# A DoRA forward pass on one core: the last stores awaited behind the closing barriers, rounding and copies in pairs, and a TensorE loop of half a block

## Chip, cores and metric

The kernel runs on one core of a Trainium2 chip. The metric is the device time of one execution in microseconds; lower is better. Four of the core's engines compute: TensorE (PE), VectorE (DVE), ScalarE (ACT) and GpSimd (POOL). SyncE (SP) issues the large transfers. "Span" is the time from the first to the last instruction of the program in a trace; every timed execution has a time and a span, and the difference ("time outside the span") matters below.

## The reference

```python
def setup_inputs():
    batch, seq_len, in_dim, out_dim = 16, 2048, 256, 256
    rank = 16
    ...
def reference(x, W, lora_A, lora_B, m, scale):
    W_adapted = W + scale * (lora_A @ lora_B)
    W_norm = np.sqrt(np.sum(W_adapted ** 2, axis=0, keepdims=True) + 1e-8)
    W_final = W_adapted / W_norm * m
    x_flat = x.reshape(-1, in_dim)           # 32768 x 256 float32
    y = x_flat @ W_final                     # 32768 x 256 float32
    return y.reshape(batch, seq_len, out_dim).astype(np.float32)
```

x and y are 33.5 MB each. The weights are tiny and are prepared once.

## The kernel before

The rows are cut into 8 blocks of 4096 (4 MB). Five buffers hold blocks; a result overwrites its input and is stored from there. A block is 8 chunks of 512 rows. For a chunk, POOL rounds to bfloat16, PE transposes (two bfloat16 values carried as one float32), DVE copies the transposed chunk out of PSUM, PE multiplies by the final weights, and ACT copies the product over the input.

SyncE issues all large loads and stores on one queue:

```python
    for b in range(XBUFS):                       # XBUFS = 5
        load_x(b)
    for b in range(NBLK):                        # NBLK = 8
        nc.sync.wait_ge(sem("done"), b + 1)
        nc.sync.dma_start(out=rows(out_flat, b), in_=x_bufs[b % XBUFS][:]).then_inc(
            sem(f"store{b}"), 16
        )
        if b >= 1 and b - 1 + XBUFS < NBLK:
            nc.sync.wait_ge(sem(f"store{b - 1}"), 16)
            load_x(b - 1 + XBUFS)
    for b in range(NBLK - XBUFS, NBLK):
        nc.sync.wait_ge(sem(f"store{b}"), 16)
    # ... [cut] after this: the closing barriers of the framework
```

A barrier is a meeting of the five engines: each signals that it has come, and waits until all have. In the trace of this kernel all five have semaphore events on the line of the closing barriers (L303), from 163.5 to 164.3 us.

POOL and DVE have one instruction per chunk (64 each); TensorE loops over blocks:

```python
    for g in range(NCH):                         # 64 chunks
        ... # [cut] waits
        nc.gpsimd.tensor_copy(out=xb_bufs[g % NXB][:],
            in_=x_bufs[b % XBUFS][:, c * J : (c + 1) * J, :]).then_inc(sem("rounded"), 1)
    # ... [cut]
    with nc.Fori(0, NBLK, 1, engines=[PE], head_slot={PE: 0}):
        turned(0)                                # 4 transposes
        for c in range(CH):                      # 8 chunks
            if c + 1 < CH:
                turned(c + 1)
            product(c)                           # 8 matmuls
```

## Time and profile before

| | before |
|---|---|
| time, median of the first three runs | 166.26 us (166.16 to 166.46) |
| span in the trace | 164.3 us |
| moved by DMA | 67.45 MB |
| busiest engine (PE) | 61% |
| last compute ends; last store issued | 139.6 us; 139.7 us |
| last store has landed | 162.8 us |

The page of the kernel before. Part 2 has one digit per fortieth of the span, 9 for 90% busy or more; below it are the GB/s of each slice.

```profile
span 164.3 us, 2075 instructions
PE 99.7 (61%) x778; PEld 83.9 (51%) x778; DVE 51.2 (31%) x76; ACT 66.8 (41%) x67; POOL 66.2 (40%) x70
...
DMA  5998999989999999999999999999999999999960
GB/s 199 415 479 383 499 391 415 479 383 495 399 399 359 399 479 401 439 439 399 479 407 439 447 399 457 433 423 455 407 431 439 423 463 399 439 447 407 471 295 16
...
q8 instruction: 1, 0.02, 0.0%
q14 instruction: 3, 0.02, 0.0%
...
L150 POOL CAST xb<-x_sb 128x1024 bf16<-128x1024 f32 x64 | 65.5, 1049 | 65.2 <-DMA x_sb<-in_x_dram 50.6
L184 DVE COPY xt<-xt_ps 128x512 f32<-128x512 f32 x64 | 43.9, 691 | 77.1 <-PE xt_ps L246 77.1
```

The DMA row stands at 8 or 9 from the second slice to the last but two, and no engine row (left out here) does. The "instruction" packets of q8 and q14 are taken to be fetches of the engines' own programs (called instruction fetches below): with TensorE's loop written out q8 has six packets in place of one, and with the main loops taken out it has none (late_unroll and dma_only, below). POOL and DVE wait for data for longer than DVE works. That is a kernel which moves bytes, and whose compute has time to spare.

SyncE's waits from 140 us on, in the kernel before (columns: total us, number, longest), and then its end by windows (us; only the last three columns matter: the granted clock of PE, the DMA engines' share, GB/s; a packet is counted whole in the window in which it starts, so a share can pass 1):

```profile
SPq L130 <- DMA out_dram<-x_sb: 22.8, 2, 13.1
SPq L303 <- PEq L303: 0.8, 2, 0.6
```

```profile
150.00:155.00 5.00, 0.00 (x0) 0.00 (x0) 0.00 (x0) 0.00 (x0) 0.00 (x0) 0.50 1.02 439
155.00:160.00 5.00, 0.00 (x0) 0.00 (x0) 0.00 (x0) 0.00 (x0) 0.00 (x0) 0.50 0.77 334
160.00:165.00 5.00, 0.00 (x0) 0.00 (x0) 0.00 (x0) 0.00 (x0) 0.00 (x0) 0.50 0.05 20
```

Three things stand here. SyncE does nothing but wait for stores up to 162.8 us. After that the barriers come (L303), in which nothing moves. And in the last 5 us the DMA engines are 5% busy: most are through by about 160 us, a few are not.

One view misleads. The chain that ended last begins and ends with compute, because its steps are compute instructions, and a store's landing is not one:

```profile
137.51 1.05 PE y_ps L258 x8
138.56 0.02 issue
138.58 1.01 ACT x_sb L201
```

It stops at 139.6 us and says nothing of the 25 us after. Where the end is a transfer, read the waits of SyncE instead.

The trace also records when each of the 16 parts of a transfer has landed. (One part per DMA engine: in this trace 16 packets are under way at a time, and 99% of those of 8 KB or more start within 4 ns of the end of an earlier one.) For the last store of the kernel before, in us:

```
159.39 159.52 159.63 159.64 159.65 159.75 159.75 159.89 159.94 159.97 160.04 160.10 160.12 160.31 162.55 162.80
```

Fourteen parts end within 0.9 us; two stragglers are 2.7 and 2.9 us behind the eighth. Below, "lag" is a part's landing minus that of the eighth part.

### The profile page before, as it was taken

The page shows a single profiled execution, that of the slowest core. Times are in us where ns is not written, and L with a number is a line of the kernel's source. Part 1 is how long each engine was busy: PE and PEld are TensorE (multiplying, and loading weights), DVE is VectorE, ACT ScalarE, POOL GpSimd, SP SyncE. Part 2 cuts the span into 40 slices and gives each one's busy share as a digit, 9 for nine tenths or more (in the row PEclk, how much of TensorE's full clock was granted, in tenths as well). Part 3 has the DMA queues.
Part 4 walks back from the last instruction along what each step waited for, and adds up shares of the span by engine and source line. Part 5 has one row for each costly group of instructions (what it writes and reads, how often), then busy time and mean ns, then how long its engine had stood idle before and what let it go on. Part 6 is the DMA issues. An engine that isn't in the chain of part 4 may idle for free. (4 is left out here: it accounts for less than half of the span.)

```text
span 164.3 us, 2075 instructions
## 1 busy us (share of the span) xinstructions
PE 99.7 (61%) x778; PEld 83.9 (51%) x778; DVE 51.2 (31%) x76; ACT 66.8 (41%) x67; POOL 66.2 (40%) x70
## 2 busy tenths in 40 slices
PE   1260899899899898994009993399704996000000
PEld 0120698798798796992007891279603895000000
DVE  0439355354453554451003450045301352000000
ACT  3010077577578577576000675027800377000000
POOL 1006859587785885800039600693007920000000
PEclk9999999999999999999555799579995799955555
DMA  5998999989999999999999999999999999999960
GB/s 199 415 479 383 499 391 415 479 383 495 399 399 359 399 479 401 439 439 399 479 407 439 447 399 457 433 423 455 407 431 439 423 463 399 439 447 407 471 295 16
DMA packets 2630, 67.45 MB, mean 410 GB/s; under 512 B 433, under 2 KB 450, under 8 KB 578
## 3 DMA queue, kind: packets, MB, share of 16 engines
q1 hardware_dynamic: 2448, 67.37, 95.9%
q10 hardware_dynamic: 178, 0.03, 0.1%
q8 instruction: 1, 0.02, 0.0%
q14 instruction: 3, 0.02, 0.0%
HBM read 33.85 MB, written 33.55 MB: 410 GB/s over the span
## 5 line engine op out<-in xcount | busy, mean ns | idle before, releaser
L150 POOL CAST xb<-x_sb 128x1024 bf16<-128x1024 f32 x64 | 65.5, 1049 | 65.2 <-DMA x_sb<-in_x_dram 50.6
L201 ACT COPY x_sb<-y_ps 128x1024 f32<-128x1024 f32 x64 | 64.8, 1013 | 64.5 <-PE y_ps L258 64.5
L258 PE MATMUL y_ps<-w_final,xt 128*128 128x256 bf16 x512 | 69.9, 282 | 3.9 <-PEq L235 3.6
L184 DVE COPY xt<-xt_ps 128x512 f32<-128x512 f32 x64 | 43.9, 691 | 77.1 <-PE xt_ps L246 77.1
L246 PE MATMUL xt_ps<-identity,xb 128*128 128x128 f32 x256 | 41.8, 295 | 28.4 <-PEq L235 28.4
L258 PEld LDWEIGHTS y_ps<-w_final,xt 128*128 128x128 bf16 x512 | 50.7, 101 | 14.7 <-issue 8.3
L246 PEld LDWEIGHTS xt_ps<-identity,xb 128*128 128x128 f32 x256 | 32.7, 153 | 31.4 <-issue 30.7
L223 PE MATMUL y_ps<-sq,ones 128*128 128x256 f32 x4 | 2.1, 674 | 1.6 <-DVE sq L169 1.6
L194 ACT ACTIVATE norm<-y_ps,eps_col 128x256 f32<-128x256 f32 x1 | 0.5, 474 | 5.9 <-PE y_ps L223 5.9
L212 PE MATMUL y_ps<-identity,a_nat 128*16 128x128 f32 x2 | 0.6, 396 | 3.6 <-DMA a_nat<-in_lora_A_dram 3.6
L180 DVE TENSOR_TENSOR w_final<-wam,rnorm 128x256 bf16<-128x256 f32 x2 | 2.3, 1200 | 0.0
L223 PEld LDWEIGHTS y_ps<-sq,ones 128*128 128x128 f32 x4 | 1.2, 323 | 2.3 <-DVE sq L169 2.1
L192 ACT ACT_TABLE_LOAD x1 | 1.3, 1283 | 2.4 <-issue 2.4
L212 PEld LDWEIGHTS y_ps<-identity,a_nat 128*16 128x16 f32 x2 | 0.1, 88 | 3.6 <-issue 3.6
L177 DVE RECIPROCAL rnorm<-norm 128x256 f32<-128x256 f32 x1 | 1.7, 1745 | 0.0
L171 DVE COPY m_all<-y_ps 128x256 f32<-128x256 f32 x1 | 0.4, 425 | 3.3 <-PE y_ps L228 3.3
L160 DVE CAST b_bf<-b_nat 16x256 bf16<-16x256 f32 x1 | 0.3, 281 | 3.6 <-DMA b_nat<-in_lora_B_dram 3.6
L216 PE MATMUL y_ps<-b_bf,aT 16*128 16x256 bf16 x2 | 0.6, 402 | 1.3 <-DVE aT L162 1.3
L228 PE MATMUL y_ps<-m_row,ones 1*128 1x256 f32 x2 | 1.2, 710 | 0.0
L216 PEld LDWEIGHTS y_ps<-b_bf,aT 16*128 16x128 bf16 x2 | 0.1, 104 | 1.8 <-DVE aT L162 1.8
L165 DVE SCALAR_TENSOR_TENSOR wa<-y_ps,w_nat 128x512 f32<-128x512 f32 x1 | 0.7, 692 | 0.8 <-PE y_ps L216 0.8
L228 PEld LDWEIGHTS y_ps<-m_row,ones 1*128 1x128 f32 x2 | 0.5, 308 | 0.7 <-issue 0.7
(12 smaller groups left out, 3.2 us busy)
## 6 DMA issues: line engine op xcount, KB each, us to landing
x_sb<-in_x_dram SPq DMA_DIRECT2D x8, 4096.0 KB, 29.3
out_dram<-x_sb SPq DMA_DIRECT2D x8, 4096.0 KB, 34.1
w_nat<-in_W_dram SPq DMA_DIRECT2D x1, 256.0 KB, 2.9
a_nat<-in_lora_A_dram ACTq DMA_DIRECT2D x1, 16.0 KB, 2.6
b_nat<-in_lora_B_dram ACTq DMA_DIRECT2D x1, 16.0 KB, 3.5
m_row<-in_m_dram ACTq DMA_DIRECT2D x1, 1.0 KB
```

What stands on the lines that cost most here:

```text
L150: nc.gpsimd.tensor_copy(out=xb_bufs[g % NXB][:], in_=x_bufs[b % XBUFS][:, c * J : (c + 1) * J, :],).then_inc(sem("rounded"), 1)
L165: nc.vector.scalar_tensor_tensor(out=wa[:], in0=ab_ps, scalar=float(scale), in1=w_nat[:], op0=ALU.mult, op1=ALU.add).then_inc(dv, 1)
L177: nc.vector.reciprocal(out=rnorm[:], in_=norm[:]).then_inc(dv, 1)
L180: i = nc.vector.tensor_mul(out=w_final[:, t], in0=wam[:, t], in1=rnorm[:])
L184: nc.vector.tensor_copy(out=xt_bufs[g % NXT][:].rearrange("p r t -> p (r t)").bitcast(FP32), in_=xt_ps[g % 4][:],).then_inc(sem("copied"), 1)
L192: nc.scalar.activation(out=warm[:], in_=eps_col[:], func=AF.Sqrt)
L201: nc.scalar.copy(out=x_bufs[b % XBUFS][:, c * J : (c + 1) * J, :], in_=y_ps[g % 2][:]).then_inc(sem("room"), 1)
L212: i = nc.tensor.transpose(aT_ps[:, t * P : (t + 1) * P], a_nat[:, t, :], identity[:])
L223: i = nc.tensor.matmul(n2_ps, ones[:], sq[:, t, :], start=(t == 0), stop=(t == KC - 1))
L228: nc.tensor.matmul(mb_ps, ones[0:1, :], m_row[:], start=True, stop=True).then_inc(pe, 1)
L246: i = nc.tensor.transpose(xt_ps[c % 4][:, j * P : (j + 1) * P], xb_bufs[c % NXB][:, j, :].bitcast(FP32), identity[:],)
L258: i = nc.tensor.matmul(y_ps[c % 2][:, j, :], xt_bufs[c % NXT][:, j * P : (j + 1) * P, t], w_final[:, t, :], start=(t == 0 and (j % (J // 2 ...
```

## The change

Its intent: the closing barriers and the semaphore clear take place under the last stores instead of after them, and POOL, DVE and TensorE need fewer, larger steps. The core of the diff:

```diff
-    ctx.enter_context(tc.tile_critical())
+    critical = ExitStack()
+    critical.enter_context(tc.tile_critical())
...
+    late = [nc.alloc_semaphore(f"store{b}") for b in range(NBLK - XBUFS, NBLK)]
+    sems = {f"store{b}": late[b - NBLK + XBUFS] for b in range(NBLK - XBUFS, NBLK)}
...
-    for b in range(NBLK - XBUFS, NBLK):
-        nc.sync.wait_ge(sem(f"store{b}"), 16)
...
-    for g in range(NCH):
+    for p in range(NPR):                     # 32 pairs of chunks
...
         nc.gpsimd.tensor_copy(
-            out=xb_bufs[g % NXB][:],
-            in_=x_bufs[b % XBUFS][:, c * J : (c + 1) * J, :],
+            out=xb_bufs[p % NXB][:],
+            in_=x_bufs[b % XBUFS][:, 2 * c * J : 2 * (c + 1) * J, :],
         ).then_inc(sem("rounded"), 1)
+    nc.gpsimd.wait_ge(sem("turned"), NPR - NXB + 1)
+    nc.gpsimd.memset(xb_bufs[NPR % NXB][:], 0.0).then_inc(sem("rounded"), 1)
... (DVE copies pairs likewise; two PSUM tiles of 1024 in place of four of 512)
-    with nc.Fori(0, NBLK, 1, engines=[PE], head_slot={PE: 0}):
+    turned(0)
+    with nc.Fori(0, NPR // 2, 1, engines=[PE], head_slot={PE: 96}):
+        turned(1)
+        product(0)
+        product(1)
         turned(0)
-        for c in range(CH):
-            if c + 1 < CH:
-                turned(c + 1)
-            product(c)
+    critical.close()
+    tc.close()
+    tc.compile()
+    for s in late:
+        nc.sync.wait_ge(s, 16)
+        nc.sync.sem_clear(s)
```

The loop now turns one pair more than there are (`turned(0)` at its end); POOL's `memset` gives it something to turn.

More of the change, by code (lines that the diff above doesn't have):

```diff
@@ L45 @@
     NCH = NBLK * CH
-    NXB = 4
-    NXT = 4
-    F4 = J * P
+    NPR = NCH // 2
+    PRB = CH // 2
+    NXB = 2
+    NXT = 2
+    F8 = 2 * J * P
     PE = mybir.EngineType.PE
-    ctx.enter_context(tc.tile_critical())
+    critical = ExitStack()
+    critical.enter_context(tc.tile_critical())
     def sb(name, shape, dtype):
@@ L62 @@
     x_bufs = [sb(f"x_sb{k}", [P, DJ, IN], FP32) for k in range(XBUFS)]
-    xb_bufs = [sb(f"xb{k}", [P, J, IN], BF16) for k in range(NXB)]
-    xt_bufs = [sb(f"xt{k}", [P, F4, KC], BF16) for k in range(NXT)]
+    xb_bufs = [sb(f"xb{k}", [P, 2 * J, IN], BF16) for k in range(NXB)]
+    xt_bufs = [sb(f"xt{k}", [P, F8, KC], BF16) for k in range(NXT)]
     w_nat = sb("w_nat", [P, KC, OUT], FP32)
@@ L82 @@
     w_final = sb("w_final", [P, KC, OUT], BF16)
-    xt_ps = [ps(f"xt_ps{k}", [P, F4], FP32) for k in range(4)]
+    xt_ps = [ps(f"xt_ps{k}", [P, F8], FP32) for k in range(2)]
     y_ps = [ps(f"y_ps{k}", [P, J, OUT], FP32) for k in range(2)]
@@ L90 @@
     mb_ps = y_ps[1][:, 2, :]
-    sems = {}
+    late = [nc.alloc_semaphore(f"store{b}") for b in range(NBLK - XBUFS, NBLK)]
+    sems = {f"store{b}": late[b - NBLK + XBUFS] for b in range(NBLK - XBUFS, NBLK)}
     def sem(name):
@@ L143 @@
     ).then_inc(sem("ident"), 1)
-    for g in range(NCH):
-        b, c = divmod(g, CH)
+    for p in range(NPR):
+        b, c = divmod(p, PRB)
         if c == 0:
             nc.gpsimd.wait_ge(sem(f"load{b}"), 16)
-        if g >= NXB:
-            nc.gpsimd.wait_ge(sem("turned"), g - NXB + 1)
+        if p >= NXB:
+            nc.gpsimd.wait_ge(sem("turned"), p - NXB + 1)
         nc.gpsimd.tensor_copy(
-            out=xb_bufs[g % NXB][:],
-            in_=x_bufs[b % XBUFS][:, c * J : (c + 1) * J, :],
+            out=xb_bufs[p % NXB][:],
+            in_=x_bufs[b % XBUFS][:, 2 * c * J : 2 * (c + 1) * J, :],
         ).then_inc(sem("rounded"), 1)
+    nc.gpsimd.wait_ge(sem("turned"), NPR - NXB + 1)
+    nc.gpsimd.memset(xb_bufs[NPR % NXB][:], 0.0).then_inc(sem("rounded"), 1)
     dv = sem("dve")
@@ L181 @@
     i.then_inc(dv, 1)
-    for g in range(NCH):
-        nc.vector.wait_ge(sem("turned"), g + 1)
+    for p in range(NPR):
+        nc.vector.wait_ge(sem("turned"), p + 1)
         nc.vector.tensor_copy(
-            out=xt_bufs[g % NXT][:].rearrange("p r t -> p (r t)").bitcast(FP32),
-            in_=xt_ps[g % 4][:],
+            out=xt_bufs[p % NXT][:].rearrange("p r t -> p (r t)").bitcast(FP32),
+            in_=xt_ps[p % 2][:],
         ).then_inc(sem("copied"), 1)
@@ L240, with turned @@
         j_order.append(a + J // 2)
-    def turned(c):
+    def turned(p):
         take("rounded")
-        for j in range(J):
+        for j in range(2 * J):
             i = nc.tensor.transpose(
-                xt_ps[c % 4][:, j * P : (j + 1) * P],
-                xb_bufs[c % NXB][:, j, :].bitcast(FP32),
+                xt_ps[p % 2][:, j * P : (j + 1) * P],
+                xb_bufs[p % NXB][:, j, :].bitcast(FP32),
                 identity[:],
@@ L251, in turned, with product @@
         i.then_inc(sem("turned"), 1)
-    def product(c):
+    def product(p):
         take("copied")
-        take("room")
-        for t in range(KC):
-            for j in j_order:
-                i = nc.tensor.matmul(
-                    y_ps[c % 2][:, j, :],
-                    xt_bufs[c % NXT][:, j * P : (j + 1) * P, t],
-                    w_final[:, t, :],
-                    start=(t == 0 and (j % (J // 2)) == 0),
-                    stop=(t == KC - 1 and (j % (J // 2)) == (J // 2) - 1),
-                )
-        i.then_inc(sem("product"), 1)
-    with nc.Fori(0, NBLK, 1, engines=[PE], head_slot={PE: 0}):
-        turned(0)
-        for c in range(CH):
-            if c + 1 < CH:
-                turned(c + 1)
-            product(c)
+        for h in range(2):
+            take("room")
+            for t in range(KC):
+                for j in j_order:
+                    r = (h * J + j) * P
+                    i = nc.tensor.matmul(
+                        y_ps[h][:, j, :],
+                        xt_bufs[p % NXT][:, r : r + P, t],
+                        w_final[:, t, :],
+                        start=(t == 0 and (j % (J // 2)) == 0),
+                        stop=(t == KC - 1 and (j % (J // 2)) == (J // 2) - 1),
+                    )
+            i.then_inc(sem("product"), 1)
+    turned(0)
[3 more added lines that the diff above has]
+        product(1)
+        turned(0)
+    critical.close()
[4 more added lines that the diff above has]
+        nc.sync.sem_clear(s)
 _INS = ['x', 'W', 'lora_A', 'lora_B', 'm', 'scale']
```

## The prediction

> **What bounds it now.** The DMA queues. The slice table has DMA at 8 or 9 tenths from 4 us to 160 us: 67.45 MB, mean 410 GB/s; 5 us windows show mostly 415 to 445 GB/s with or without compute beside them. In the landing records, the successive 4 MB transfers land 9.5 to 10.5 us apart. The engines are far below: PE 61%, ACT 41%, POOL 40%, DVE 31%. The last block's compute ends at 139.6 us (timeline), while the store that it releases can only begin to move when the store ahead is through, at about 150 us: 10 us of slack.
>
> **The tail.** SyncE waits for the last store until 162.8 us (waits of SP, L130). Then come the branch, two sets of barriers over five engines and a semaphore range clear of 0.24 us, to 164.3 us: 1.45 us in which nothing moves. About 1.9 us more of the 166.26 lie outside the span.
>
> **A second loss in the tail.** 14 of 16 engines have landed the last store by 160.3 us; two straggle to 162.55 and 162.80. The first lag (1.4 us) appears with the transfer during which the queue table's one "instruction" packet of q8 moved 16 KB (20.4 us); the second engine's lag grows from 53 us on, by about 0.3 us around each of the three 8 KB instruction fetches of q14 (65, 99 and 106 us).[...]
>
> **What the change does.**
> 1. Waits of the last stores behind the barriers: barriers and range clear run at about 140 us, under the stores. After the landing only a wait and a clear of SyncE remain, about 0.03 us each as the tail's waits show. Gain: 1.2 to 1.4 us, all on the critical path.
> 2. Pairs: 32 rounds of about 2.0 us (twice 1049 ns) and 32 copies of about 1.3 us (twice 691 ns). Pipeline steps get twice as coarse: the last block, 15.5 us from its load's landing to its last store's issue, should take 16 to 20 us, within its 25 us. Off the critical path: 0.
> 3. PE loop of 48 instead of 96 matmuls with the next pair turned ahead: PE is 61% busy: 0.
> 4. Side effect: shorter streams (half the POOL and DVE instructions, half the PE loop body), so fewer or earlier instruction fetches among the data. If the 16 KB fetch goes or moves before the loads, a straggler loses 1.4 us; but the other stays at about +2 us unless its fetches go too. I expect 0 to 1 us, 0.5 us in the middle.
>
> **Sum.** 166.26 - 1.35 - 0.5 = 164.4 us, 1.1% faster. Eight times in ten between 163.3 and 165.3. Chances: faster 0.06, same 0.93, slower 0.01.
>
> **What would show it.** SP's wait for the last store at the end, no barrier behind it; barriers near 140 us; end of span within 0.2 us of the last landing; POOL x32 at about 2.0 us, DVE x32 at about 1.3 us; compute end between 139 and 145 us. Step 4: fewer "instruction" packets, the stragglers closer to the other 14.
>
> **What would make it wrong.** The last block's compute later than about 150 us (PE at half clock throughout), which would open a gap before the last store; a straggler that grows instead; or time outside the span changing as SyncE ends last.

## The result, and the profile after

The median is 164.62 us (164.47 to 164.74, 4 runs) against 166.35 us (166.16 to 166.46, 4 runs) for the kernel before. The ratio is 0.9897, with a 95% interval of 0.9879 to 0.9914. A ratio here is the mean time of one kernel's fast runs over that of the other's of the same rounds, so it is not quite the ratio of the quoted medians.

The page of the changed kernel, the same lines:

```profile
span 163.3 us, 1983 instructions
PE 103.6 (63%) x786; PEld 84.2 (52%) x786; DVE 43.9 (27%) x44; ACT 63.6 (39%) x67; POOL 62.2 (38%) x39
...
DMA  5999998999999999999999999999999999999991
GB/s 201 394 490 401 425 470 385 482 417 393 482 409 361 401 401 482 401 450 433 409 466 409 401 490 393 442 452 401 474 409 393 474 409 433 458 401 474 409 393 48
...
q8 instruction: 1, 0.02, 0.0%
q14 instruction: 1, 0.01, 0.0%
...
L154 POOL CAST xb<-x_sb 128x2048 bf16<-128x2048 f32 x32 | 59.7, 1893 | 70.9 <-DMA x_sb<-in_x_dram 49.8
L191 DVE COPY xt<-xt_ps 128x1024 f32<-128x1024 f32 x32 | 38.1, 1221 | 86.6 <-PE xt_ps L253 86.6
```

Pairs save 5.8 us of POOL's rounding and 5.8 us of DVE's copying, and both engines simply wait longer (POOL's new memset takes 1.8 us of it back). SyncE's waits in the changed kernel from 143 us on, and its last windows:

```profile
SPq L129 <- ACTq L212: 19.9, 1, 19.9
SPq L289 <- DMA out_dram<-x_sb: 18.5, 2, 9.6
SPq L286 <- PEq L286: 0.7, 2, 0.5
```

```profile
150.00:155.00 5.00, 0.00 (x0) 0.00 (x0) 0.00 (x0) 0.00 (x0) 0.00 (x0) 0.50 0.99 426
155.00:160.00 5.00, 0.00 (x0) 0.00 (x0) 0.00 (x0) 0.00 (x0) 0.00 (x0) 0.50 0.77 334
160.00:165.00 5.00, 0.00 (x0) 0.00 (x0) 0.00 (x0) 0.00 (x0) 0.00 (x0) 0.50 0.06 26
```

The barriers (L286) now run at 143.3 to 144.6 us and the wait for stores (L289) comes last. The span ends 0.04 us after the last landing (163.28 and 163.24 us), where it ended 1.5 us after it before (164.31 and 162.80). The middle of the run is unchanged: the first part of the last store landed at 159.39 us in both traces. The chain of the changed kernel's trace is as blind as before; it ends with ACT's last copies:

```profile
139.89 1.05 PE y_ps L267 x8
140.93 0.02 issue
140.96 1.93 ACT x_sb L208 x2
```

The last block took 18.4 us from its load's landing (124.51 us) to its store's issue (142.94 us), against 15.6 us before, and nothing came of it.

Two things didn't fit, though the total did. The last straggler landed 0.44 us later than before (163.24 against 162.80 us), not earlier, and a third part lagged in this trace (161.77 us). And the span fell by 1.0 us between the two traces while the median time fell by 1.7 us. (In the two traced executions alone the time fell by 1.35 us, from 166.09 to 164.74 us, so only a part of the 0.7 us lies outside the span; the means below put it at 0.36 us.) These two were the questions for the experiments.

### The profile page after: what moved, and what is told of

It is laid out like the page before. It is cut to its first block, busy times and chain, and to the rows that moved or that the text cites. A ratio compares the mean times of both kernels' runs of the same rounds, so it can differ in the third digit from the quotient of the medians.

```text
span 163.3 us, 1983 instructions
## 1 busy us (share of the span) xinstructions
PE 103.6 (63%) x786; PEld 84.2 (52%) x786; DVE 43.9 (27%) x44; ACT 63.6 (39%) x67; POOL 62.2 (38%) x39
## 5 line engine op out<-in xcount | busy, mean ns | idle before, releaser
L208 ACT COPY x_sb<-y_ps 128x1024 f32<-128x1024 f32 x64 | 61.7, 1014 | 71.7 <-PE y_ps L267 71.7
L154 POOL CAST xb<-x_sb 128x2048 bf16<-128x2048 f32 x32 | 59.7, 1893 | 70.9 <-DMA x_sb<-in_x_dram 49.8
L267 PE MATMUL y_ps<-w_final,xt 128*128 128x256 bf16 x512 | 63.3, 276 | 13.4 <-PEq L242 13.4
L267 PEld LDWEIGHTS y_ps<-w_final,xt 128*128 128x128 bf16 x512 | 47.8, 99 | 28.0 <-issue 19.9
L191 DVE COPY xt<-xt_ps 128x1024 f32<-128x1024 f32 x32 | 38.1, 1221 | 86.6 <-PE xt_ps L253 86.6
L253 PE MATMUL xt_ps<-identity,xb 128*128 128x128 f32 x264 | 38.7, 307 | 20.0 <-PEq L242 20.0
L253 PEld LDWEIGHTS xt_ps<-identity,xb 128*128 128x128 f32 x264 | 34.5, 159 | 22.8 <-issue 22.6
L160 POOL MEMSET xb<- 128x2048 bf16 x1 | 1.8, 1804 | 3.8 <-PE xt_ps L253 3.8
L187 DVE TENSOR_TENSOR w_final<-wam,rnorm 128x256 bf16<-128x256 f32 x2 | 0.8, 422 | 0.0
```

The lines of the kernel that those rows point to most:

```text
L154: nc.gpsimd.tensor_copy(out=xb_bufs[p % NXB][:], in_=x_bufs[b % XBUFS][:, 2 * c * J : 2 * (c + 1) * J, :],).then_inc(sem("rounded"), 1)
L160: nc.gpsimd.memset(xb_bufs[NPR % NXB][:], 0.0).then_inc(sem("rounded"), 1)
L187: i = nc.vector.tensor_mul(out=w_final[:, t], in0=wam[:, t], in1=rnorm[:])
L191: nc.vector.tensor_copy(out=xt_bufs[p % NXT][:].rearrange("p r t -> p (r t)").bitcast(FP32), in_=xt_ps[p % 2][:],).then_inc(sem("copied"), 1)
L208: nc.scalar.copy(out=x_bufs[b % XBUFS][:, c * J : (c + 1) * J, :], in_=y_ps[g % 2][:]).then_inc(sem("room"), 1)
L253: i = nc.tensor.transpose(xt_ps[p % 2][:, j * P : (j + 1) * P], xb_bufs[p % NXB][:, j, :].bitcast(FP32), identity[:],)
```

## The experiments

Theory 1: the late waits are the whole gain, in two parts, the barriers inside the span and something outside the span that the other four engines do while SyncE still waits. Rivals: pairs and the shorter loop bring a part of the gain through shorter programs or fewer instruction fetches. For the stragglers the theory was that an instruction fetch of TensorE takes time from one DMA engine; the rivals were compute in general, and the DMA engines themselves.

The first four ran on one chip in the same rounds. All outputs were correct unless stated.

### Late waits alone (late_only)

```diff
 # the kernel before, with only:
-    for b in range(NBLK - XBUFS, NBLK):
-        nc.sync.wait_ge(sem(f"store{b}"), 16)
 ... (at the end, as in the change)
+    critical.close(); tc.close(); tc.compile()
+    for s in late:
+        nc.sync.wait_ge(s, 16); nc.sync.sem_clear(s)
```

> The kernel before with only the waits for the last five stores moved behind the closing barriers. Theory 1 (the late waits are the whole gain): ratio to before 0.988 to 0.991, about 164.5 us, the span ends within 0.1 us of the last landing, and time minus span falls from about 1.95 us to about 1.45 us as in the changed kernel. Rival (pairs and the shorter loop bring a part of it, through shorter programs or fewer instruction fetches): only the barriers' 1.4 us come off, ratio about 0.992 or more, time minus span stays at about 1.95 us.

Measured: 164.32 us (164.03 to 164.63, 4 runs), ratio 0.9889 (0.9867 to 0.9910). Theory 1 held. SyncE's waits in its trace have the barriers ahead of the stores, as in the changed kernel, and its last landing is at 162.68 us:

```profile
SPq L279 <- DMA out_dram<-x_sb: 21.7, 3, 9.7
SPq L276 <- PEq L276: 0.7, 2, 0.5
```

### Pairs and the half-block loop alone (pairs_only)

```diff
 # the changed kernel, with:
+    for b in range(NBLK - XBUFS, NBLK):
+        nc.sync.wait_ge(sem(f"store{b}"), 16)     # inside, ahead of the barriers
-    for s in late: ...                            # and nothing behind them
```

> The changed kernel with its waits for the stores back in front of the barriers: only pairs and the half-block loop remain. Theory 1: within 0.3% of before (165.9 to 166.8 us), time minus span about 1.95 us, last compute 2 to 4 us later than before without effect. Rival: faster than before by 0.3% or more, with time minus span of about 1.45 us.

Measured: 166.62 us (166.43 to 166.90, 5 runs), ratio 1.0018 (0.9999 to 1.0036). Theory 1 held: no gain. If there is an effect it is a loss of 0.2%.

### The other four engines held until the last store has landed (all_late)

```diff
 # the changed kernel, and at its very end:
+    others = (nc.tensor, nc.vector, nc.scalar, nc.gpsimd)
+    for e, s in zip(others, fins):
+        nc.sync.sem_inc(s, 1)
+    for e, s in zip(others, fins):
+        e.wait_ge(s, 1)
+        e.sem_clear(s)
```

> The changed kernel, but PE, DVE, ACT and POOL are held after the barriers until SyncE has seen the last store; then each goes on. If time minus span falls in the changed kernel because those four engines finish what comes after the program's last instruction under the stores, this run gets it back: time minus span about 1.95 us, time about 0.5 us plus some 0.1 us of semaphores over the changed kernel, 165.1 to 165.4 us. If it falls for another reason, the time is at most 0.15 us over the changed kernel (164.5 to 164.9 us).

Measured: 165.74 us (165.51 to 165.95, 5 runs), ratio 0.9961 (0.9943 to 0.9979), 1.06 us over the changed kernel's median. The direction is as the theory said, the size is more: time outside the span came back entirely, and 0.2 us on top (2.14 us against 1.92 us with pairs alone; table below). The span grew by 0.36 us as well. The surplus stays unexplained; this trace alone has an 8 KB instruction fetch after the end of the span, which may belong to the added instructions.

### The changed kernel again (after_again)

> The changed kernel as it is, for comparison in the same rounds: 164.4 to 164.8 us, ratio 0.989 to 0.991. The last store's landing shows again how much the stragglers vary between traces of one kernel: if by 0.4 us or more, the 0.44 us by which they were later in its first trace than in that of before means nothing.

Measured: 164.68 us (164.35 to 164.85, 4 runs), ratio 0.9902 (0.9879 to 0.9925). Its last landing was at 163.15 us, 0.09 us from that of its first trace, so the later straggler is not a matter of one trace; that other kernels' traces spread more is said below.

The four together, means of the fast runs of these rounds in us; the last column is the mean of (time minus span):

| kernel | time | span | outside the span |
|---|---|---|---|
| before (9 runs) | 166.27 | 164.48 | 1.80 |
| late waits alone | 164.32 | 163.00 | 1.32 |
| pairs and loop alone | 166.64 | 164.72 | 1.92 |
| both (the changed kernel) | 164.64 | 163.20 | 1.44 |
| both, four engines held | 165.70 | 163.56 | 2.14 |

The parts add up: late waits -1.95 us, pairs and loop +0.37 us, sum -1.58 us, measured together -1.63 us. Late waits take 1.48 us from the span and 0.48 us from outside it. No trace here records what the engines do outside the span. What these runs show is only this: when four engines may leave early, 0.48 us go, and when they are held, 0.70 us come back (2.14 against 1.44).

The next four ran on one chip in the same rounds, built on the late waits alone.

### TensorE's loop written out (late_unroll)

```diff
 # late waits alone, with:
-    with nc.Fori(0, NBLK, 1, engines=[PE], head_slot={PE: 0}):
+    for _ in range(NBLK):
```

> The kernel with the late waits alone (164.3 us), its TensorE loop written out: some 1730 TensorE instructions[...]. Theory (each 16 KB instruction page takes about 1.3 us from one and the same DMA engine, and the last store waits for that engine): 5 to 6 more fetches, last landing 6 to 8 us later, time 170 to 173 us. Rival (the 1.3 us lag at 20 us is not the fetch's doing, or fetches fall on different engines): last landing and time within 1.5 us of the looped kernel.

Measured: 164.40 us (164.09 to 164.50, 4 runs), ratio 0.9879 (0.9862 to 0.9895). Six instruction packets of 16 KB were fetched (at 36, 50, 64, 76, 112 and 133 us) in place of one, and the time did not move. The theory as I put it, one and the same DMA engine for all fetches, fell. But the stragglers did change: no part lagged at 20 us any more, the first lag of 1.70 us came with the first fetch at 36 us, and at the end more parts were late, none much later:

```
last six parts of the last store, us
loop:     160.22 160.24 160.28 160.40 162.55 162.68
unrolled: 160.96 161.41 161.85 162.19 162.28 162.95
```

So a fetch comes with a delay of the DMA engine that it falls on (1.70 us of lag here, 1.5 us in the trace of before), and the fetches fall on different engines. The traces don't name engines, but each packet starts within a few ns of the end of the one before on its engine: followed in this way, the fetches at 50, 64, 76 and 133 us stand on engines whose last packets end at four different times (160.04, 161.52, 161.94 and 160.52 us).

### Transfers without compute (dma_only)

```diff
 # late waits alone, with:
-        nc.sync.wait_ge(sem("done"), b + 1)
+        nc.sync.wait_ge(sem(f"load{b}"), 16)
 # and the main loops of POOL, DVE, ACT and PE taken out (the output is x, wrong on purpose)
```

> Wrong on purpose: with the late waits, the same loads and stores in the same order, each store after its load, and no rounding, transposes, products or copies, so the output is x. Theory (DMA alone sets the time, and compute only adds the stragglers' lag through TensorE's page fetch): the first parts land at the same times within 0.3 us (159.4 to 159.7 for the last store), the jump of 1.3 us of one engine during the second load is gone, time 162 to 164 us. Rival 1 (compute slows the transfers[...]): first part of the last store lands before 158 us, time under 161 us. Rival 2 (stragglers are the DMA engines' own): stragglers as before, 164.0 to 164.6 us. It also shows whether all engines' slow packets at 49 to 51 us come from compute.

Measured: 162.97 us as the median of all four runs, one of which was slow; the fast three were 162.10 to 163.12 us; ratio of the fast runs 0.9764 (0.9737 to 0.9791). The theory held (the first part by 0.01 us outside its range): the first part of the last store landed at 159.71 us, as with compute (159.39 us in the traces of before and of the changed kernel), so compute does not slow the transfers as a whole. The lag of the second load is gone (0.34 us, against 1.52 us in the late waits alone), and the last part of the last store lagged by 1.59 us instead of about 2.7 to 3.6. Rival 2, the DMA engines' own, has the remaining 1.6 us.

### The last block delayed (slack7)

```diff
 # late waits alone, ahead of the last block's rounding:
+        if g == NCH - CH:
+            for k in range(7):
+                nc.gpsimd.tensor_copy(out=waste[:], in_=...same chunk...)
+                    .then_inc(sem("wasted"), 1)
+                nc.gpsimd.wait_ge(sem("wasted"), k + 1)
```

> The kernel with the late waits alone, with 7 more roundings of about 1.05 us each ahead of the last block, into an unused tile: the last store is issued about 7.3 us later, at about 147 us. Theory (10 us of slack before the last block): no change, 164.0 to 164.7 us. Rival (the last block's compute is on the path): up to 7 us slower; 1 us or more would count for it.

Measured: 164.71 us (164.38 to 165.36, 4 runs), ratio 0.9903 (0.9874 to 0.9932). The last store was issued at 147.61 us instead of 139.19 us:

```profile
147.61 0.33 SPq L126 DMA_DIRECT2D out_dram<-x_sb  x1
```

A delay of 8.4 us in the last block's compute came with some 0.4 us (mean 164.79 against 164.34 us for the unrolled kernel of the same rounds, whose runs overlap with these; the late waits alone were not run on this chip), and the first part of the last store landed at 159.60 us all the same. The slack is there. The 0.4 us are in the stragglers again (last lag 3.42 us); I can't say why.

### The last store cut up (probe)

```diff
 # late waits alone, the last store as seven transfers:
+            rows 0..27 of all 128 partitions, then rows 28..31 of partitions
+            (16, 128), (0, 8), (8, 12), (12, 14), (14, 15), (15, 16), a semaphore each
```

> The kernel with the late waits alone, the last store cut up to find the lagging engines: rows 0 to 27 of all partitions as one transfer, then the last 4 rows as transfers of 112, 8, 4, 2, 1 and 1 partitions, each with its own semaphore.[...] Time about 164.3 us plus up to 1 us for the six issues.

Measured: 165.57 us in one run, of unknown state; only its landings are used. The number of landings follows the number of partitions: 9 for 8 partitions (one at the issue, then 8), 5 for 4, 3 for 2. The landings don't name engines; which engines a small transfer runs on was my assumption, and no run here shows it. The transfer of 8 partitions had one part at 163.37 us, with the next at 161.09; that of 4 partitions ended at 161.28. So one part in eight lagged by 2.28 us in the first, no part of the second landed as late, and the latest landing of all (163.91 us) is in the 112-partition transfer. Which engines lag stays open.

The last four ran on one chip: late_again, rebalance and store_first in one set of rounds, rebalance4 after them, beside one more run of the kernel before.

### Late waits alone, again (late_again)

> The kernel before with the late waits alone, again, as the measure for the next two in the same rounds: 164.1 to 164.7 us, ratio 0.987 to 0.990.

Measured: 164.06 us (163.88 to 164.28, 5 runs), ratio 0.9877 (0.9860 to 0.9893).

### Less of the last store for the laggards (rebalance)

```diff
 # as the cut-up store: rows 0..27 of all, then rows 28..31 of partitions
+            (0, 49), (49, 84), (84, 119), (119, 126), (126, 128)
```

The division rests on my assumption about which engines a small transfer runs on. Two cases were put down: the laggards have less to move and the store ends earlier, or a laggard has more and it ends later.

> The late waits alone, and the last store divided: 28 of 32 rows on all 16 engines, the last 4 rows as transfers of 49, 35, 35, 7 and 2 partitions.[...] last landing at about 161.6 to 162.0 us instead of 162.7, time 163.2 to 163.8 us, 0.6 to 1.0 us under the late waits alone.[...] the 49-partition transfers land last, at 164 us or later, and the time rises by 1 us or more.

Measured: 165.14 us (165.07 to 165.79, 6 runs), ratio 0.9940 (0.9926 to 0.9954): 1.1 us slower than late_again. The second case, the later end, came true. The main part of the store was through at 161.93 us, but the small ones ended at 162.65, 163.42, 164.19 and 164.38 us. That a laggard was given more is my reading; on which engines the small transfers ran is not shown.

### The first store ahead of the fifth load (store_first)

```diff
 # late waits alone, with:
-    for b in range(XBUFS):
+    for b in range(XBUFS - 1):
         load_x(b)
 ...
+        if b == 0:
+            load_x(XBUFS - 1)      # after store 0
```

> The late waits alone, and the first store issued before the fifth load instead of after it (queue order load 0 to 3, store 0, load 4, store 1). All kernels so far, with and without compute, had two slow packets on every engine at 49 to 51 us, about 1 us lost, just ahead of the first store's data. If that belongs to the first store, it moves to 39 to 42 us; if it belongs to the time or to the number of packets moved, it stays at 49 to 51 us. The time should be the same either way, 164.0 to 164.8 us, unless the loss vanishes (then 1 us less).

Measured: 164.65 us (164.20 to 165.21, 4 runs), ratio 0.9907 (0.9881 to 0.9933). The slow stretch moved with the first store. The windows of late_again first, then those of store_first (the last two columns: DMA share, GB/s):

```profile
40.00:45.00 5.00, 4.26 (x38) 3.56 (x37) 1.99 (x4) 3.05 (x4) 3.08 (x4) 1.00 0.97 419
45.00:50.00 5.00, 5.00 (x48) 4.66 (x47) 2.53 (x5) 3.82 (x5) 3.93 (x5) 1.00 1.03 419
50.00:55.00 5.00, 4.26 (x38) 3.55 (x37) 2.47 (x4) 3.42 (x4) 3.28 (x4) 1.00 0.89 315
```

```profile
40.00:45.00 5.00, 4.26 (x38) 3.56 (x37) 1.99 (x4) 3.04 (x4) 3.08 (x4) 1.00 0.89 315
45.00:50.00 5.00, 5.00 (x48) 4.67 (x47) 2.53 (x5) 3.82 (x5) 3.93 (x5) 1.00 0.97 419
50.00:55.00 5.00, 4.26 (x39) 3.56 (x37) 2.39 (x4) 3.33 (x4) 3.28 (x4) 1.00 0.99 426
```

The 315 GB/s come just ahead of the first store's data, and they are there without compute too (315 GB/s at 50 to 55 us in the trace of the transfers alone). In the trace of before, 28 packets, 27 of them of 1.3 to 2.1 us and one of 3.0 us, in place of 1.21 us make up 16.8 us, or on average 1.05 us for each of 16 engines; the eighth part of the fifth load, the last ahead of that store, landed 0.8 us later than the 9.71 us between loads would give. Nothing is gained by the order; the loss is paid once either way. The mean was 0.58 us above that of late_again, with runs that just overlap (164.20 against 164.28 us): the worst straggler lagged by 3.56 us at the end, against 2.72 us.

### Less for the laggards, second try (rebalance4)

```diff
 # as the cut-up store: rows 0..29 of all, then rows 30..31 of partitions
+            (0, 124), (124, 128)
```

> The late waits alone, the last store divided once more: 30 of 32 rows on all 16 engines, the last 2 rows as transfers of 124 and 4 partitions.[...] last landing at 162.0 to 162.4 us instead of 162.7, time 163.4 to 163.9 us, 0.3 to 0.6 us under the late waits alone (ratio 0.984 to 0.987). If pieces of 2 KB are slower than their bytes[...], the small transfers land last, after 162.7 us, and the time is that of the late waits alone or more.

Measured: 164.08 us (163.83 to 164.32, 4 runs), ratio 0.9875 (0.9855 to 0.9894): the same as late_again. The main part landed at 162.61 us, the small ones at 162.58 and 162.76 us. The second case again, but not by the small pieces alone. A 2 KB packet took 84 ns at best, 24 GB/s, where a full-size packet of 32 KB takes 1.213 us, 27 GB/s; so 31 such packets one after another, 124 partitions on four engines by my assumption, which is not shown, would take an estimated 2.6 us at least (31 times 84 ns). And the laggard was further behind in this trace: 3.10 us at the store before the last, against 2.71 us in late_again, so that the main part landed only 0.1 us earlier than late_again's last (162.72 us).

No version tried beats the late waits alone, measured at 164.32 and 164.06 us. In the same rounds it was 0.3 us faster than the changed kernel (means 164.32 against 164.64 us), though their runs overlap. So it is at least as good, with less changed.

## Why the prediction was right, point by point

The time (164.62 us, predicted 164.4, range 163.3 to 165.3) was right. Not every term of the sum was.

| term | predicted, us | measured, us | by |
|---|---|---|---|
| barriers behind the stores, in the span | -1.35 | -1.48 | late_only against before, spans |
| outside the span | 0, named as a risk | -0.48 | the same runs, time minus span; all_late |
| pairs, loop, fewer fetches | 0 and -0.5 | +0.37 | pairs_only against before |
| sum | -1.85 | -1.58; both together -1.63 | |

1. *What bounds the kernel.* Right. Without compute the transfers took as long up to the first part of the last store (159.71 us), and 8.4 us of delay in the last block came with some 0.4 us, which the runs hardly tell from nothing.
2. *Step 1, the barriers.* Right in mechanism and nearly in size. The prediction missed that engines freed early also save time outside the span (0.48 us); it named that span-external time as a risk without a number.
3. *Steps 2 and 3, pairs and the loop.* Right in the profile: 1.89 us and 1.22 us (predicted about 2.0 and 1.3), 18.4 us for the last block (16 to 20), compute's end within 139 to 145 us. They gained nothing; there may be a loss of 0.2%.
4. *Step 4, fewer fetches.* This is the term that failed. Two of the three 8 KB fetches did go, but the stragglers did not move up: in the two traces of the changed kernel the last part landed at 163.24 and 163.15 us, against 162.80 us before. The 16 KB fetch did not go at all (20.43 us in the changed kernel). And the 8 KB fetches were not what the stragglers waited for. The prediction put the second straggler's growth down to them, some 0.3 us each; but with one such fetch in place of three it ended 2.51 and 2.79 us behind the eighth part, against 2.66 us before. The packets show why: on one DMA engine each starts within a few ns of the end of the one before (99% within 4 ns, in the trace of before), so an engine's packets can be followed to the end. In the trace of before the three 8 KB fetches fell on three engines, cost them 0.4 to 0.7 us each (a fetch of 0.31 us, then a packet of 1.33 to 1.56 us in place of 1.21), and these engines' last packets ended at 159.7 to 159.9 us; the stragglers' ended at 162.1 and 162.5 us. Fewer fetches were read as fewer costs without asking on which engine they fall.

The failed term was 0.87 us off by the means (-0.5 predicted, +0.37 measured); the term without a number (-0.48) and the 0.13 us more from the barriers made up for 0.61 us of that. So it is in part luck that the total agreed. The total alone would have passed for a proof of all four steps. Only the runs with one part each told them apart.

How the 16 KB fetch shows, from the landing records: the last part's lag in us, at the first and the second load (and the fourth, where it matters).

| trace | first 16 KB fetch | lag of load 0 | lag of load 1 |
|---|---|---|---|
| before | 20.44 us | 0.15 | 1.56 |
| late waits alone | 19.18 us | 0.44 | 1.52 |
| pairs and loop alone | 20.83 us | 0.39 | 1.93 |
| changed kernel | 20.43 us | 0.28 | 1.49 |
| unrolled | 36.32 us (load 3: 1.70) | 0.22 | 0.24 |
| transfers alone | none | 0.36 | 0.34 |

The lag comes with the fetch, moves with it, and is absent without it. In the trace of before, the fetch's packet took 0.98 us, and the packet after it 1.71 instead of 1.21 us: 1.5 us in all. Another part of the worst straggler's lag came in the slow stretch ahead of the first store (see store_first): in the trace of before the last part lagged by 1.58 us at the fourth load and by 2.60 us at the fifth, and the one packet of 3.0 us stands there; in store_first, where the stretch comes one load earlier, by 2.03 us at the third load and 3.23 us at the fourth. The transfers alone have the stretch without that step (0.34 and 0.24 us).

What stays open: why the pairs' last straggler is about half a microsecond later than without pairs (163.45 us in pairs_only; 162.68 and 162.72 us in the two traces of the late waits alone), what the second straggler's slow growth from 53 us on comes from, and what exactly lies in the 0.48 us outside the span. Stragglers also drifted in kernels that have no pairs (last landings at 163.50 us in slack7 and 163.54 us in store_first), so the first may be no property of pairs at all.

## What to carry to other kernels

When one resource is full from start to finish, look at its two ends: what runs before it starts and after it stops is what a change elsewhere can win, apart from what it takes of the resource itself (here the engines' own instruction fetches: the 16 KB one came with a lag of 1.1 to 1.5 us more in one part of 16, by the table above). Work that needs no transferred data (closing barriers, semaphore clears, engines that could leave) belongs under the last transfer, not after it; here that was 1.95 of 166.3 us, and reshaping compute with 10 us of slack was worth nothing. And when a total agrees with a forecast, still run each part alone, since two wrong terms can cancel.
